# A decoder block on one core: the feed-forward entry written out in a fixed order with its weights split early, and the first score products shared

## The chip, the cores and the metric

The kernel runs on one core of a Trainium2 chip. The metric is device time in microseconds (us). Five engines run side by side, each with its own instruction stream: PE (TensorE, matmuls and transposes), ACT (ScalarE), DVE (VectorE), POOL (GpSimd) and SP (SyncE, which here issues nearly all DMAs). Semaphores tie them together. An engine works its stream in order, so an instruction that waits holds up all that stands behind it.

## The reference, cut to what matters

One decoder block on 512 tokens of width 1024: a norm, one combined projection, sparse attention beside an mLSTM, an output projection, and a feed-forward part with hidden width 4096. All in float32. The change touches the attention scores of the selected and of the window branch, and the feed-forward part:

```
s_s = einsum('bqghd,bqgnkd->bqghnk', qc, k_sel) + bias_s    # selected branch
p_s = masked_softmax(s_s, dist_s >= 0)
s_w = einsum('bqghd,bkgd->bqghk', qc, kwc) + bias_w         # window branch
p_w = masked_softmax(s_w, mask_w)
...
x = x + mixed @ w_out[l]
h2 = rms_norm(x, norm2_g[l])
x = x + square(relu(h2 @ w_ff1[l])) @ w_ff2[l]
```

With 512 tokens both branches see every earlier token, so the kernel computes both as causal attention over the whole sequence, with their own keys and values.

## The kernel before

**Matmuls in two halves.** A float32 operand is stored as a high part and a low part. `split` (L119) makes them: ACT writes the high part, then DVE subtracts it from the source and writes the low part. `mm3` (L114) multiplies them with three matmuls: high by high (L115), high by low (L116), low by high (L117). So every operand passes ACT and then DVE before its product can end.

**Attention.** There are 16 units: 8 heads, two branches each. `Unit.scores(qt)` multiplies 128 queries with their 128·(qt+1) keys, high and low part. For qt = 0 the product is 256 columns wide though 128 keys are needed. DVE then adds the bias and takes the row's extreme (`P`), and ACT takes the exponential. Work on the other branch (the "fill" stream) stands between these steps on PE. Once, between units, `cmp_scores(1)` (products `sc`, copied by ACT to `sT`, transposed to `sct` on PE) stands there too.

**Feed-forward entry.** After `out_proj`, DVE adds the residual (`x`), POOL takes a root, DVE writes `hn`, and `norm2_T(tt)` transposes one tile of 128 tokens in 8 PE transposes into `tpn`; `normed_T` splits them into `hT_h` and `hT_l` and copies them whole into `hF`. The token tiles 0 and 1 are done within `out_proj`, 2 and 3 within the first products. `first_ff1` computes the hidden blocks f = 0 to 3 directly: for tokens 0 to 255 four blocks of 24 matmuls, then the same for tokens 256 to 511, 192 matmuls of 256 columns in all. Then come relu, square and the split into `u`.

**Pairs of blocks.** From f = 4 on, two blocks at a time are computed by seven products (`do1` to `do7` in `products`) of 12 matmuls each, in place of eight. They take sums of token parts (T1 to T4, made from `hF` by three subtractions in `tokens`, a fourth for T4) and sums of weight parts (the forms a, s, t, b, made from `w1r` through `w1s` on DVE and then split). The products accumulate in four PSUM banks X, Y, Z and W. `do1` writes X, and ACT copies it out (`p1`, in the tile `g2`); `do5` adds to X and must wait for that copy. `do2` to `do4` leave sums in `g2` and `hn` on DVE. The second feed-forward matrix is applied in units of three 512-column matmuls, which `merge` sets between the products.

**What sets the order.** PE's order is the order in which the code is written (a manual schedule). The order on ACT, DVE, POOL and SP is chosen by a scheduler from its own estimates. In `mix` the numbers are times in the PE stream at which an event (such as `norm2_T(3)`) is put in. Buffers in a pool are reused in turn: a DMA into a `w1raw` or `w1r` tile waits until the last reader of that buffer is done.

Of the kernel before, what the change touches and what calls it, by code (L numbers as in the profile page):

```python
# [52 lines left out]
def hybrid_block_kernel(  # L53
# [91 lines left out]
    def normed_T(hn, tt, tags, full=None):  # L145
        for k0 in (0, 4):
# [705 lines left out]
    class Unit:  # L852
# [7 lines left out]
        def scores(self, qt):  # L860
            h, br = self.h, self.br
            if qt == 0:
                if br == 0:
                    for hn in ((h, h + 1) if h == 0 else (h + 1,)):
                        if hn < H:
                            bts[hn] = load_bias(hn)
                self.l = wk.tile([128, TT], F32, name="l4", bufs=3)
                self.nx = wk.tile([128, TT], F32, name="nx", bufs=3)
# [4 lines left out]
            nc.tensor.matmul(st[:, :m], qv, ks[:, br, 0, self.g, :m], start=True, stop=False)  # L873
            nc.tensor.matmul(st[:, :m], qv, ks[:, br, 1, self.g, :m], start=False, stop=True)  # L874
            P = wk.tile([128, n], F32, name="P", tag=f"P{qt}", bufs=3)
            c0 = 384 - 128 * qt
            V.tensor_tensor_reduce(P, st[:, :n], bts[h][:, c0:c0 + n], -1.0, 3e38, ALU.add, ALU.min,  # L877
# [148 lines left out]
    with pool("ffa") as fa, pool("ffr") as fr, pool("ffu") as fu, pool("fft") as ft:  # L1026
        UB = 13
        us = {}

        def utile(name, dt=F32R):  # L1030
            return fu.tile([128, 2 * S], dt, name=name, tag="u", bufs=UB)

        def ev_u(f, r):

            u = utile("u").rearrange("p (a t) -> p a t", a=2)
# [4 lines left out]
        def load_first(f):  # L1040
            parts = []
            for k in (0, 4):
                raw = fr.tile([128, 4, 256], F32, name="w1raw", tag="raw", bufs=2)
                nc.sync.dma_start(raw, w_ff1[:, k:k + 4, 128 * f:128 * f + 256])
                h, l = (utile("w1" + c).rearrange("p (k c) -> p k c", k=4) for c in "hl")
# [4 lines left out]
        def first_ff1():  # L1050

            ws = [load_first(0), load_first(2)]
            ps_ = [acc("pj", ("pj", "o")[f // 2], 2) for f in range(4)]
            for hs in (slice(0, 256), slice(256, 512)):
                for f in range(4):
                    for k in range(KT):
                        mm3(ps_[f][:, hs], *ws[f // 2](k, slice(128 * (f % 2), 128 * (f % 2) + 128)),
                            hT_h[:, k, hs], hT_l[:, k, hs], k == 0, k == KT - 1)
                        yield 3 * 256 / 2400
# [8 lines left out]
        def tokens():  # L1068
# [5 lines left out]
            for i, t in ((2, b22), (1, b11), (3, b12)):  # L1074
                T[i] = [ft.tile([128, 4, 256], F32R, name=f"T{i}{c}") for c in "hl"]
                split(*T[i], t)
            V.tensor_sub(b21, b21, b22)

            T[4] = [hT_h[:, 0:4, lo_], hT_l[:, 0:4, lo_]]

        def tokens4():
            split(*T[4], hF[1][:, :, hi_])
# [9 lines left out]
        def w1_load(f, first=False):  # L1092
            if first:
                raw, ss = ([utile(n, F32).rearrange("p (k c) -> p k c", k=4) for _ in range(2)] for n in ("w1r", "w1s"))
# [27 lines left out]
        def products(f, w, nxt):  # L1122
# [70 lines left out]

        def w2_load(i):
            if i < len(tiles2) and tiles2[i] not in w2s:
                c, ch, f = tiles2[i]
                raw = fr.tile([128, 2, S], F32, name="w2r", tag="raw", bufs=2)
                nc.sync.dma_start(raw, w_ff2[:, 8 * c + f:8 * c + f + 2, 512 * ch:512 * ch + 512])
                h, l = (fa.tile([128, 2, S], F32R, name="w2" + n, bufs=2) for n in "hl")
# [32 lines left out]
        def first_pair():  # L1232
            w = w1_load(4, first=True)
# [60 lines left out]
```

## Time and profile before

| | us |
|---|---|
| three runs | 810.63 to 811.78, median 811.16 |
| profiled execution | 809.97 |
| its span | 808.2 |
| PE busy | 787.5 (97%) |
| DVE busy | 536.3 (66%) |
| ACT busy | 407.3 (50%) |

The span is what the profile covers; 1.77 us of the profiled execution lie outside it. The profiled execution is 1.19 us below the median of the runs. A row of the timeline gives the start of an instruction, its length, its engine, its line and its operands; matmuls overlap in the pipeline, so what a matmul costs is the distance from its start to the next start, not its length.

### The profile page before, as it was taken

The page shows a single profiled execution, that of the slowest core. Times are in us where ns is not written, and L with a number is a line of the kernel's source. Part 1 is how long each engine was busy: PE and PEld are TensorE (multiplying, and loading weights), DVE is VectorE, ACT ScalarE, POOL GpSimd, SP SyncE. Part 2 cuts the span into 40 slices and gives each one's busy share as a digit, 9 for nine tenths or more (in the row PEclk, how much of TensorE's full clock was granted, in tenths as well). Part 3 has the DMA queues.
Part 4 walks back from the last instruction along what each step waited for, and adds up shares of the span by engine and source line. Part 5 has one row for each costly group of instructions (what it writes and reads, how often), then busy time and mean ns, then how long its engine had stood idle before and what let it go on. Part 6 is the DMA issues. An engine that isn't in the chain of part 4 may idle for free.

```text
span 808.2 us, 12445 instructions
## 1 busy us (share of the span) xinstructions
PE 787.5 (97%) x4772; PEld 697.3 (86%) x4772; DVE 536.3 (66%) x1007; ACT 407.3 (50%) x746; POOL 71.4 (9%) x150
## 2 busy tenths in 40 slices
PE   6999999999999999999999989999999999999998
PEld 5978889998888888888888789999998999989886
DVE  6689796778676657764754588677665767664332
ACT  6556564554466656664423576445444444444311
POOL 2000000322122221321000000000000000000000
PEclk9999999999999999999999999999999999999999
DMA  8633231666132123212332241423233333331141
GB/s 308 195 105 92 65 105 49 191 209 182 53 92 79 52 67 92 65 53 79 124 135 68 65 157 56 137 95 105 83 101 105 105 105 105 105 105 53 53 153 56
DMA packets 66320, 84.91 MB, mean 105 GB/s; under 512 B 4063, under 2 KB 50471, under 8 KB 66132
## 3 DMA queue, kind: packets, MB, share of 16 engines
q1 hardware_dynamic: 66168, 84.03, 33.2%
q8 instruction: 37, 0.61, 0.3%
q14 instruction: 23, 0.19, 0.1%
q10 hardware_dynamic: 92, 0.09, 0.0%
HBM read 81.98 MB, written 4.75 MB: 107 GB/s over the span
## 4 chain that ended last, share of the span: by engine, by line
PE 89%; DMA 4%; DVE 3%; ACT 2%; issue 1%; POOL 1%; SPq 0%; DVEq 0%; ACTq 0%; POOLq 0%
PE pj L115 18%; PE pj L116 18%; PE pj L117 18%; PE fo L115 7%; PE fo L117 7%; PE fo L116 7%; PE ao L911 3%; PE tpP L894 2%; PE st L874 1%; PE st L873 1%; DMA bt<-rel_d 1%; DMA w2r<-in_w_ff_dram 1%; PE tpn L149 1%; PE mo L431 1%; PE mo L430 1%
## 5 line engine op out<-in xcount | busy, mean ns | idle before, releaser
L115 PE MATMUL fo<-w2h,u 128*128 128x512 f32 x256 | 100.9, 394 | 0.0
L117 PE MATMUL fo<-w2h,u 128*128 128x512 f32 x256 | 100.2, 391 | 0.0
L116 PE MATMUL fo<-w2l,u 128*128 128x512 f32 x256 | 100.0, 391 | 0.0
L115 PE MATMUL pj<-whi,hT_h 128*128 128x256 f32 (+2 forms) x288 | 84.3, 293 | 3.5 <-ACT hT_h L120 1.8
L105 DVE TENSOR_TENSOR wlo<-wraw,whi 128x1024 fp32r<-128x1024 f32 (+2 forms) x58 | 72.1, 1243 | 21.7 <-ACT whi L104 20.7
L117 PE MATMUL pj<-whi,hT_l 128*128 128x256 f32 (+2 forms) x288 | 82.2, 286 | 0.0
L116 PE MATMUL pj<-wlo,hT_h 128*128 128x256 f32 (+2 forms) x288 | 81.9, 284 | 0.0
L115 PE MATMUL pj<-hT_h,whi 128*128 128x512 f32 x192 | 80.7, 420 | 0.4 <-DVE vv L121 0.4
L116 PE MATMUL pj<-hT_l,whi 128*128 128x512 f32 x192 | 75.9, 395 | 0.0
L117 PE MATMUL pj<-hT_h,wlo 128*128 128x512 f32 x192 | 75.7, 395 | 0.0
L104 ACT CAST whi<-wraw 128x1024 fp32r<-128x1024 f32 (+2 forms) x58 | 60.9, 1050 | 27.9 <-PE pj L116 12.7
L121 DVE TENSOR_TENSOR w2l<-w2r,w2h 128x1024 fp32r<-128x1024 f32 x32 | 39.2, 1223 | 50.1 <-ACT w2h L120 50.1
L120 ACT ACTIVATE w2h<-w2r 128x1024 fp32r<-128x1024 f32 x32 | 33.9, 1060 | 60.9 <-PE fo L117 60.9
L115 PEld LDWEIGHTS pj<-whi,hT_h 128*128 128x128 f32 x288 | 55.1, 191 | 5.0 <-ACT hT_h L120 2.1
L117 PEld LDWEIGHTS fo<-w2h,u 128*128 128x128 f32 x256 | 48.1, 188 | 11.1
L116 PEld LDWEIGHTS pj<-wlo,hT_h 128*128 128x128 f32 x288 | 55.2, 192 | 0.1
L117 PEld LDWEIGHTS pj<-whi,hT_l 128*128 128x128 f32 x288 | 55.0, 191 | 0.1
L116 PEld LDWEIGHTS fo<-w2l,u 128*128 128x128 f32 x256 | 48.3, 189 | 6.6
L115 PEld LDWEIGHTS fo<-w2h,u 128*128 128x128 f32 x256 | 48.2, 188 | 6.6
L877 DVE CUSTOM_DVE_ANT_0 P<-st,bt 128x128 f32<-128x128 f32 (+1 forms) x64 | 31.1, 486 | 28.5 <-PE st L874 26.2
L120 ACT ACTIVATE ph<-tpP 128x512 fp32r<-128x512 f32 (+1 forms) x64 | 27.8, 435 | 43.2 <-PE tpP L894 42.6
L887 POOL TENSOR_SCALAR P<-P,l 128x128 f32<-128x128 f32 (+1 forms) x64 | 34.2, 553 | 110.5 <-DVE l L885 110.5
(334 smaller groups left out, 2111.7 us busy)
## 6 DMA issues: line engine op xcount, KB each, us to landing
wraw<-in_w_in_dram SPq DMA_DIRECT2D x38, 512.0 KB, 3.8
w2r<-in_w_ff_dram SPq DMA_DIRECT2D x32, 512.0 KB, 3.7
w1r<-in_w_ff_dram SPq DMA_DIRECT2D x28, 512.0 KB, 4.8
bt<-rel_d SPq DMA_DIRECT2D x16, 256.0 KB, 2.9
wraw<-in_w_out_dram SPq DMA_DIRECT2D x8, 512.0 KB, 3.7
rel_d<-rel_r SPq DMA_DIRECT2D x1, 2560.0 KB
x<-in_x_dram SPq DMA_DIRECT2D x4, 512.0 KB, 8.2
wraw<-in_cmp_k_w_dram SPq DMA_DIRECT2D x8, 256.0 KB, 3.5
```

What stands on the lines that cost most here:

```text
L104: nc.scalar.copy(hi[:, :n], raw[:, :n])
L105: nc.vector.tensor_sub(lw[:, :n], raw[:, :n], hi.bitcast(F32)[:, :n])
L115: nc.tensor.matmul(o, ah, bh, start=start, stop=False, **kw)
L116: nc.tensor.matmul(o, ah, bl, start=False, stop=False, **kw)
L117: nc.tensor.matmul(o, al, bh, start=False, stop=stop, **kw)
L120: nc.scalar.activation(h, src, AF.Copy, scale=scale)
L121: nc.vector.tensor_sub(l, src, h.bitcast(F32))
L149: nc.tensor.transpose(tp[:, k * 128:(k + 1) * 128], hn[:, (k0 + k) * 128:(k0 + k + 1) * 128], ident)
L877: V.tensor_tensor_reduce(P, st[:, :n], bts[h][:, c0:c0 + n], -1.0, 3e38, ALU.add, ALU.min, self.nx[:, qt:qt + 1])
L887: nc.gpsimd.tensor_scalar(self.P[i], self.P[i], self.l[:, i:i + 1], 1.0, op0=ALU.mult, op1=ALU.mult)
L894: nc.tensor.transpose(tp[:, (qt - kt) * 128:(qt - kt + 1) * 128], self.P[qt][:, kt * 128:(kt + 1) * 128], ident)
L911: nc.tensor.matmul(o[:, S - x_.shape[-1]:], vn[:, self.br, self.g, kt, :], x_, start=self.br == 0 and kt == 0 and i == 0, stop=False)
```

## The change

It has two parts.

First, the score products of qt = 0 are shared. The product was 256 columns wide with 128 of use; now the selected branch's unit multiplies the queries with the first 128 keys of both branches at once, and the window branch's unit has no product for qt = 0. The part behind the product becomes a function, `soft`; for the window branch it is called at once, with the selected branch's, four steps earlier than before.

Second, the feed-forward entry. The raw weights for f = 0 to 3 and the weights of the first pair (f = 4) get buffers of their own and are loaded and split ahead of the products; `normed_T` copies the transposes whole to `hF` first and splits from that copy; the first block of `first_ff1` runs its 16 products with the high weights before its 8 with the low weights; `norm2_T(3)` stands 24 matmuls or so earlier in PE's stream; token sums, token forms and weight forms are events between the matmuls; w1's forms a and s for the next pair move from `do3` to `do4`; a load and a split of w2 are separate calls; the first pair is merged with 6 units from `do5` on, the second with 10. From here to the end of the first pair, ACT and DVE too run in the order in which the code is written.

```diff
-            split(hT_h[sl], hT_l[sl], tp.rearrange("p (k t) -> p k t", k=4))
+            t = tp.rearrange("p (k t) -> p k t", k=4)
             if full is not None:
-                nc.scalar.copy(full[k0 // 4][:, :, sl[2]], tp.rearrange("p (k t) -> p k t", k=4))
+                f = full[k0 // 4][:, :, sl[2]]
+                nc.scalar.copy(f, t)
+                t = f
+            split(hT_h[sl], hT_l[sl], t)
...
+            if qt == 0 and br == 1:
+                return
...
+            for i in range(2):
+                kv = ks[:, :, i, self.g, :n] if qt == 0 else ks[:, br, i, self.g, :n]
+                nc.tensor.matmul(st[:, :m], qv, kv, start=i == 0, stop=i == 1)
+            self.soft(qt, st[:, :n])
+            if qt == 0:
+                us[2 * h + 1].soft(qt, st[:, n:m])
...
+                    if f or hs.start:
+                        for k in range(KT):
+                            mm3(o, *wk_[k], hT_h[:, k, hs], hT_l[:, k, hs], k == 0, k == KT - 1)
+                            yield 3 * 256 / 2400
+                    else:
+                        for k in range(KT):
+                            nc.tensor.matmul(o, wk_[k][0], hT_h[:, k, hs], start=k == 0, stop=False)
+                            nc.tensor.matmul(o, wk_[k][0], hT_l[:, k, hs], start=False, stop=False)
+                            yield 2 * 256 / 2400
+                        for k in range(KT):
+                            nc.tensor.matmul(o, wk_[k][1], hT_h[:, k, hs], start=False, stop=k == KT - 1)
+                            yield 256 / 2400
...
             def do3():
                 prod(Z, "s1", 1, True)
                 V.tensor_add(t5, Z, u2)
+
+            def do4():
+                prod(W_, "t3", 3, True)
+                V.tensor_add(r[:, 1, lo_], W_, t5)
                 if w:
                     w1_a(w)
                     w1_s(w)
-
-            def do4():
-                prod(W_, "t3", 3, True)
-                V.tensor_add(r[:, 1, lo_], W_, t5)
...
-                for j in range(i, i + 2):
-                    w2_load(j)
+                w2_load(i + 2)
+                w2_split(i + 1)
...
-        mix(Stream(first_ff1()), [(1.54, lambda: norm2_T(2)), (7.32, after_norm), (11.0, first_pair),
-                                  (21.0, lambda: load_next(6)), (21.1, tokens4)])
+        ws = [load_first(0), load_first(2)]
+        w4 = w1_load(4, [tile4k("w1s", False, F32).rearrange("p (k c) -> p k c", k=4) for _ in range(2)]
+                     + [raw4k("w1r") for _ in range(2)])
+        ET = mybir.EngineType
+        es_start = ExitStack()
+        es_start.enter_context(tc.manual_schedule(engines={ET.PE, ET.Activation, ET.DVE}))
+        mix(Stream(first_ff1(ws)),
+            [(1.54, lambda: norm2_T(2)), (2.0, do((w1_a, w4), (w1_s, w4))),
+             (6.4, lambda: norm2_T(3)), (8.0, do((token_sums,), (token_form, 2), (token_form, 1))),
+             (12.0, do((w1_t, w4), (token_form, 3))), (15.6, do((w1_b, w4), (w2_load, 0), (w2_load, 1))),
+             (21.0, do((load_next, 6), (token_form, 4)))])
...
+                if lead and i == 2:
+                    w2_split(0)
...
-        merge((4, 6), 16, 3)
+        merge((4,), 6, 4)
+        es_start.close()
+        merge((6,), 10)
```

SP, from `out_proj`'s last weight loads on: `w1raw` are the raw weights for f = 0 to 3, `xr` the residual input, `w1r` the raw weights of the pair f = 4. Before:

```order
L103 DMA wraw_4953<-in_w_out_dram 128x2x512 [waits DMAHW7_49,DMAHW4_49,DVE_49]
L1044 DMA w1raw_5163<-in_w_ff1_dram 128x4x256
L1044 DMA w1raw_5169<-in_w_ff1_dram 128x4x256 [waits DMAHW1_49,DVE_49]
L1001 DMA xr_4881<-in_x_dram 128x512 [waits DMAHW2_49,DVE_49]
L1001 DMA xr_4911<-in_x_dram 128x512 [waits DVE_49]
L1001 DMA xr_4965<-in_x_dram 128x512 [waits DMAHW2_49,DVE_49]
L103 DMA wraw_4959<-in_w_out_dram 128x2x512 [waits DMAHW5_49,DVE_49]
L1001 DMA xr_5002<-in_x_dram 128x512 [waits DMAHW6_49,DMAHW3_49,DVE_49]
L1001 DMA xr_5039<-in_x_dram 128x512 [waits DMAHW7_49,DMAHW4_49,DVE_49]
```

After:

```order
L103 DMA wraw_4929<-in_w_out_dram 128x2x512 [waits DMAHW7_49,DMAHW4_49,DVE_49]
L1063 DMA w1raw_5139<-in_w_ff1_dram 128x4x256 [waits PE_49]
L1063 DMA w1raw_5145<-in_w_ff1_dram 128x4x256 [waits DMAHW1_49]
L1063 DMA w1raw_5151<-in_w_ff1_dram 128x4x256 [waits DMAHW2_49,DMAHW0_49,DVE_49]
L1063 DMA w1raw_5157<-in_w_ff1_dram 128x4x256 [waits DMAHW1_49,DVE_49]
L1016 DMA xr_4857<-in_x_dram 128x512 [waits DVE_49]
L1016 DMA xr_4887<-in_x_dram 128x512 [waits DMAHW5_49,DVE_49]
L1128 DMA w1r_5165<-in_w_ff1_dram 128x4x256 [waits DMAHW6_49,DMAHW2_49,DVE_49]
L1128 DMA w1r_5166<-in_w_ff1_dram 128x4x256 [waits DMAHW7_49,DMAHW3_49,DVE_49]
L1016 DMA xr_4941<-in_x_dram 128x512 [waits DMAHW4_49,DVE_49]
```

All four `w1raw` loads and the first pair's `w1r` loads now stand among the `xr` loads of `out_proj`; before, two of the four stood behind the last `xr`.

ACT, from the relu of block f = 2 on (before) and from the high part of form b on (after): `hn` with L1062 or L1091 is the relu of a block of `first_ff1`, `u` its high part, `hT_h<-hF` the high part of T4, `g2<-pj` the copy p1 of the bank X. Before:

```order
L1062 ACTIVATE hn_5445<-pj_5189 128x512 [waits DVE_49,PE_49]
L1036 ACTIVATE hn_5445<-hn_5445 128x512 [waits Activation_49]
L120 ACTIVATE u_5447<-hn_5445 128x512 [waits Activation_49]
L120 ACTIVATE T2h_5295<-hF_5052 128x1024 [waits DVE_49]
L1062 ACTIVATE hn_5475<-pj_5190 128x512 [waits DVE_49,PE_49]
L1145 COPY g2_5491<-pj_5487 128x256 [waits PE_49]
L1036 ACTIVATE hn_5475<-hn_5475 128x512 [waits Activation_49]
L120 ACTIVATE hT_h_83<-hF_5052 128x4x256 [waits DVE_49]
```

After:

```order
L120 ACTIVATE fbh_5397<-w1r_5166 128x1024 [waits DMAHW7_49]
L1091 ACTIVATE hn_5426<-pj_5173 128x512 [waits DVE_49,PE_49]
L1055 ACTIVATE hn_5426<-hn_5426 128x512 [waits Activation_49]
L120 ACTIVATE u_5428<-hn_5426 128x512 [waits Activation_49]
L1091 ACTIVATE hn_5456<-pj_5174 128x512 [waits DVE_49,PE_49]
L1055 ACTIVATE hn_5456<-hn_5456 128x512 [waits Activation_49]
L120 ACTIVATE u_5458<-hn_5456 128x512 [waits Activation_49]
L120 ACTIVATE hT_h_83<-hF_5028 128x4x256 [waits DVE_49]
L1174 COPY g2_5473<-pj_5469 128x256 [waits PE_49]
L120 ACTIVATE w2h_5514<-w2r_5401 128x1024 [waits DMAHW4_49,DMAHW3_49,DMAHW5_49,DMAHW2_49,DMAHW0_49]
```

The copy p1 stood one row behind the last relu and ahead of T4's high part; now it stands behind that block's square, its `u` and T4's high part, which waits for DVE.

DVE, at the change from the pair f = 4 to the pair f = 6: `u_5604`, `u_5634` (before) and `u_5614` (after) are low parts of f = 4's results, `fbl` is the low part of form b for f = 6, which `do5` of f = 6 reads, `g2_5653` and `g2_5637`, `hn_5638` belong to the products of f = 6. Before:

```order
L1176 TENSOR_TENSOR hn_5492<-pj_5490,g2_5491 128x256 [waits PE_49]
L121 TENSOR_TENSOR u_5604<-hn_5492,u_5604 128x512 [waits Activation_49]
L121 TENSOR_TENSOR fbl_5639<-w1r_5481,fbh_5638 128x1024 [waits Activation_49]
L121 TENSOR_TENSOR u_5634<-hn_5492,u_5634 128x512 [waits DVE_49,Activation_49]
L1149 TENSOR_TENSOR g2_5653<-pj_5650,g2_5653 128x256 [waits PE_49]
L1115 TENSOR_TENSOR w1s_5643<-w1r_5642 128x4x128 [waits DMAHW3_49]
L121 TENSOR_TENSOR fal_5704<-w1r_5642,fah_5703 128x512 [waits Activation_49]
```

After:

```order
L121 TENSOR_TENSOR w2l_5687<-w2r_5554,w2h_5686 128x1024 [waits DMAHW1_49,Activation_49]
L1178 TENSOR_TENSOR g2_5637<-pj_5634,g2_5637 128x256 [waits DVE_49,Activation_49]
L1182 TENSOR_TENSOR g2_5637<-pj_5635,g2_5637 128x256 [waits DVE_49,PE_49]
L1186 TENSOR_TENSOR hn_5638<-pj_5636,g2_5637 128x256 [waits DVE_49,PE_49]
L121 TENSOR_TENSOR u_5614<-hn_5474,u_5614 128x512 [waits Activation_49]
L121 TENSOR_TENSOR fbl_5619<-w1r_5462,fbh_5618 128x1024 [waits Activation_49]
L1144 TENSOR_TENSOR w1s_5623<-w1r_5622 128x4x128 [waits DMAHW4_49]
```

The low part of form b stood ahead of the first sum of f = 6's products; now it stands behind three of them, the last of which (`hn_5638`) needs `do4` of f = 6.

## Rows read from the trace of the kernel before

Each row stands as the profile gives it; times are microseconds from the start of the span unless marked ns. Within a group, a line of dots stands for rows left out.

**Rows 1.** The page: busy time (part 1); the chain by engine (part 4)

```profile
PE 787.5 (97%) x4772; PEld 697.3 (86%) x4772; DVE 536.3 (66%) x1007; ACT 407.3 (50%) x746; POOL 71.4 (9%) x150
...
PE 89%; DMA 4%; DVE 3%; ACT 2%; issue 1%; POOL 1%; SPq 0%; DVEq 0%; ACTq 0%; POOLq 0%
```

**Rows 2.** PE timeline, 456 to 489: start, duration, engine line op [idle<-releaser]

```profile
456.67 0.40 PE L117 MATMUL pj<-whi,mx_l 128*128 128x512 f32 x1
...
458.98 0.39 PE L117 MATMUL pj<-hT_h,w1l 128*128 128x256 f32 x1 [1.21 <-DVE w1l L121]
...
468.71 1.04 PE L149 MATMUL tpn<-ident,hn 128*128 128x128 f32 x8
469.50 0.36 PE L115 MATMUL pj<-hT_h,w1h 128*128 128x256 f32 x1
...
472.65 0.28 PE L117 MATMUL pj<-hT_h,w1l 128*128 128x256 f32 x1
...
475.35 0.39 PE L116 MATMUL pj<-hT_l,w1h 128*128 128x256 f32 x1 [1.74 <-DVE hT_l L121]
...
475.69 0.32 PE L115 MATMUL pj<-hT_h,w1h 128*128 128x256 f32 x1
...
479.22 0.28 PE L117 MATMUL pj<-hT_h,w1l 128*128 128x256 f32 x1
...
488.18 0.28 PE L115 MATMUL pj<-hT_h,fah 128*128 128x256 f32 x1
```

**Rows 3.** Windows: length, busy by engine, PEclk, DMA share, GB/s

```profile
457.00:459.00 2.00, 0.59 (x4) 0.32 (x3) 1.89 (x3) 1.33 (x4) 0.00 (x0) 1.00 0.00 0
...
476.00:477.00 1.00, 1.00 (x7) 1.00 (x6) 1.00 (x2) 0.99 (x3) 0.00 (x0) 0.50 0.07 16
```

**Rows 4.** Timeline of PE, 240.8 to 241: one pair of score products

```profile
240.84 0.28 PE L873 MATMUL st<-ks,qy 128*128 128x256 f32 x1
240.96 0.28 PE L874 MATMUL st<-ks,qy 128*128 128x256 f32 x1
```

**Rows 5.** Timeline of ACT, 309 to 315

```profile
309.15 0.39 ACT L879 ACTIVATE P<-P,nx 128x128 f32<-128x128 f32 x1
...
314.25 0.58 ACT L814 COPY sT<-sc 128x512 f32<-128x512 f32 x1
```

**Rows 6.** Timeline of PE, 314.8 to 315

```profile
314.88 0.66 PE L820 MATMUL sct<-ident,sT 128*128 128x128 f32 x4
```

**Rows 7.** Timeline of DVE, 420 to 421

```profile
420.28 0.69 DVE L1007 SCALAR_TENSOR_TENSOR x<-pj,xr 128x512 f32<-128x512 f32 x1 [5.71 <-PE pj L117]
```

**Rows 8.** Timeline of PE, 421.4 to 421.6

```profile
421.48 0.40 PE L115 MATMUL pj<-whi,mx_h 128*128 128x512 f32 x1
```

**Rows 9.** Timeline of SP, 413 to 414

```profile
413.02 1.02 SPq L1044 DMA_DIRECT2D w1raw<-in_w_ff_dram  x2
```

**Rows 10.** The page, DMA issues (part 6): KB each, us to landing

```profile
w1r<-in_w_ff_dram SPq DMA_DIRECT2D x28, 512.0 KB, 4.8
```

**Rows 11.** Timeline of DVE, 460 to 462: the norm of token tile 3

```profile
460.74 1.41 DVE L143 SCALAR_TENSOR_TENSOR hn<-x,nr,g 128x512 f32<-128x512 f32 x2
```

**Rows 12.** Timeline of ACT, 479 to 490

```profile
479.89 0.60 ACT L1062 ACTIVATE hn<-pj 128x512 f32<-128x512 f32 x1 [2.31 <-PE pj L117]
...
481.73 1.04 ACT L120 ACTIVATE T1h<-hF 128x1024 fp32r<-128x1024 f32 x1
...
489.79 0.37 ACT L1145 COPY g<-pj 128x256 f32<-128x256 f32 x1 [0.82 <-PE pj L117]
```

**Rows 13.** Timeline of DVE, 478 to 496

```profile
478.68 1.22 DVE L1071 TENSOR_TENSOR hF<-hF 128x1024 f32<-128x1024 f32 x1
...
482.09 0.68 DVE L121 TENSOR_TENSOR u<-hn,u 128x512 fp32r<-128x512 f32 x1
...
495.22 0.41 DVE L1149 TENSOR_TENSOR g<-pj,g 128x256 f32<-128x256 f32 x1
```

More of the change, by code (lines that the diff above doesn't have):

```diff
@@ L872, in scores, with soft @@
             qv = qs[h // 2][:, h % 2, qt * 128:(qt + 1) * 128]
[L873 to L875 removed]
+            for i in range(2):
[4 more added lines that the diff above has]
+                us[2 * h + 1].soft(qt, st[:, n:m])
+        def soft(self, qt, st):
+            h, br = self.h, self.br
+            n = 128 * (qt + 1)
+            if qt == 0:
+                self.l = wk.tile([128, TT], F32, name="l4", bufs=4)
+                self.nx = wk.tile([128, TT], F32, name="nx", bufs=4)
+            P = wk.tile([128, n], F32, name="P", tag=f"P{qt}", bufs=4 if qt == 0 else 3)
             c0 = 384 - 128 * qt
[L877 removed]
+            V.tensor_tensor_reduce(P, st, bts[h][:, c0:c0 + n], -1.0, 3e38, ALU.add, ALU.min,
                                    self.nx[:, qt:qt + 1])
@@ L1019, in hybrid_block_kernel, with tile4k, raw4k @@
     es_ring.close()
-    with pool("ffa") as fa, pool("ffr") as fr, pool("ffu") as fu, pool("fft") as ft:
-        UB = 13
+    with pool("ffa") as fa, pool("ffw") as fw, pool("ffv") as fv, pool("fft") as ft:
         us = {}
-        def utile(name, dt=F32R):
-            return fu.tile([128, 2 * S], dt, name=name, tag="u", bufs=UB)
+        def tile4k(name, first, dt=F32R):
+            p_, n = (fw, 8) if first else (fv, 5)
+            return p_.tile([128, 2 * S], dt, name=name, tag="u", bufs=n)
+        def raw4k(name):
+            return fw.tile([128, 4, 256], F32, name=name, tag="raw", bufs=2)
         def ev_u(f, r):
-            u = utile("u").rearrange("p (a t) -> p a t", a=2)
+            u = tile4k("u", (f + 8) % 13 < 8).rearrange("p (a t) -> p a t", a=2)
             nc.scalar.activation(r, r, AF.Square)
@@ L1042, in load_first @@
             for k in (0, 4):
-                raw = fr.tile([128, 4, 256], F32, name="w1raw", tag="raw", bufs=2)
+                raw = raw4k("w1raw")
                 nc.sync.dma_start(raw, w_ff1[:, k:k + 4, 128 * f:128 * f + 256])
-                h, l = (utile("w1" + c).rearrange("p (k c) -> p k c", k=4) for c in "hl")
+                h, l = (tile4k("w1" + c, True).rearrange("p (k c) -> p k c", k=4) for c in "hl")
                 split(h, l, raw)
@@ L1073, in tokens, with token_form @@
             V.tensor_sub(b22, b22, b11)
[L1074 to L1082, printed above, removed]
+        def token_form(i):
+            if i == 4:
+                V.tensor_sub(hF[1][:, :, hi_], hF[1][:, :, hi_], hF[1][:, :, lo_])
+                T[4] = [hT_h[:, 0:4, lo_], hT_l[:, 0:4, lo_]]
+            else:
+                T[i] = [(fa if (i, c) == (3, "h") else ft).tile([128, 4, 256], F32R, name=f"T{i}{c}") for c in "hl"]
+            split(*T[i], {1: hF[0][:, :, hi_], 2: hF[1][:, :, lo_], 3: hF[0][:, :, lo_], 4: hF[1][:, :, hi_]}[i])
         forms = {}
@@ L1090, in form, with w1_load @@
             forms[key] = h, l
-        def w1_load(f, first=False):
-            if first:
-                raw, ss = ([utile(n, F32).rearrange("p (k c) -> p k c", k=4) for _ in range(2)] for n in ("w1r", "w1s"))
+        def w1_load(f, tiles=None):
+            if tiles:
+                ss, raw = tiles[:2], tiles[2:]
             else:
@@ L1192, in hybrid_block_kernel, with w2_split @@
         tiles2 = [(c, ch, f) for c in range(4) for ch in range(2) for f in range(0, 8, 2)]
+        w2r = {}
         def w2_load(i):
-            if i < len(tiles2) and tiles2[i] not in w2s:
+            if i < len(tiles2):
                 c, ch, f = tiles2[i]
-                raw = fr.tile([128, 2, S], F32, name="w2r", tag="raw", bufs=2)
+                w2r[i] = raw = raw4k("w2r").rearrange("p (f k) c -> p f (k c)", f=2)
                 nc.sync.dma_start(raw, w_ff2[:, 8 * c + f:8 * c + f + 2, 512 * ch:512 * ch + 512])
-                h, l = (fa.tile([128, 2, S], F32R, name="w2" + n, bufs=2) for n in "hl")
+        def w2_split(i):
+            if i < len(tiles2):
+                raw = w2r.pop(i)
+                h, l = (t.tile([128, 2, S], F32R, name="w2" + n, bufs=2) for t, n in ((fa, "h"), (ft, "l")))
                 split(h, l, raw)
```

25 lines of the change are left out of this document (9 added, 16 removed).

## Prediction

> **What bounds the kernel now.** I read the page first: PE is busy for 97% of the span, and 89% of the chain that ended last is PE [rows 1]. So time comes from two sources only: fewer or shorter matmuls, and less waiting on PE. The timeline of PE then shows where it waits; nearly all of it lies at the feed-forward entry [rows 2]. The last matmul of the output projection starts at 456.67. At about 0.12 us for 256 columns [rows 4] and twice that for 512, the first product could start at 456.90. The first of its matmuls that needs a low weight starts only at 458.98, released by DVE. A second stop begins at 472.65: the matmul that needs the low part of token tile 3 starts at 475.35, again released by DVE. Then the granted clock is 0.50, the lower of the two levels (1.2 GHz), in the second window [rows 3]: from 475.69 to 479.22 PE starts 17 matmuls in 3.53 us, where full speed takes 17 × 0.118 = 2.01. That costs 1.52. In the first window, with the first stop, it is 1.00. The first matmul of `do1` starts at 488.18. The work between is 192 matmuls × 0.118 = 22.66 and two groups of 8 transposes at 469.50 − 468.71 = 0.79 each, 24.24 together, so it could start at 481.14. All stops of the entry together, the low clock among them, cost 488.18 − 481.14 = 7.04. This is the largest gain open to the change.
>
> **Shared score products.** Eight heads lose one pair of 256-column products each, 16 × 0.118 = **−1.89** [rows 4]. All of it is on the path, since PE has no wait there. No other work is removed: the second half of the product was computed before and thrown away.
>
> What is moved is the softmax step of the window branch for qt = 0: one step on DVE and one on ACT (0.39 on ACT [rows 5]) come four steps earlier. This is free as long as ACT and DVE have slack. At one place they have none: `sT` is copied by ACT from 314.25 to 314.83 [rows 5], and the transposes that read it start at 314.88 [rows 6]. Just ahead of it the two extra steps now stand in the chain from `P` over `ay` and `qy` to `sT`. Bounds: nothing, if the copy slips ahead; two steps of 0.39, so 0.8, if both lie in the chain. I take **+0.7**, near the upper end, because the rows leave 0.05 of slack.
>
> **Weights loaded and split early.** All four `w1raw` loads now go out in `out_proj`, and their splits (ACT 1.04, DVE 1.22 each [rows 12, 13]) lie under matmuls there. ACT and DVE have room. What can be hurt is the residual add: on DVE it stands behind the low half of the second `w1raw`. Before, this add ran from 420.28 to 420.97 [rows 7], and the bank that it frees was wanted at 421.48 [rows 8], so there is 0.51 of slack. The two loads were issued between 413.02 and 414.04 [rows 9]; with the 4.8 us of such a load [rows 10] the second lands at about 418.5, its split ends at about 420.8, the add at about 421.5, just as the bank is wanted. Bounds: 0, and one split late, 1.2. I take **+0.3**. The `xr` loads that stand behind on SP wait for buffers that come free with these adds anyway.
>
> **First blocks at full rate.** With low weights at hand, the first stop goes (458.98 less 456.90 and two matmuls, 1.84). For token tile 3, `hn` is written by DVE from 460.74 to 462.15 [rows 11]; its transposes move from 468.71 to about 464.8, after 64 matmuls less the earlier stops. One copy and two splits later, its last low half is ready at about 468.7 (ACT 0.6 and DVE 0.68 a step, one step held by form s). The first half of the products ends at about 469.85. So the second stop goes too, and with it the low clock: `do1` starts at 481.14, **−7.04**. That is counted as if the entry started at 456.90 as before; the terms above shift it as a whole.
>
> **What is late next.** This is the point of the change. The preparation of the pair is one chain over ACT and DVE, and it is now in written order. I add it up with the rows' prices [rows 12, 13]: 1.22 for 1024 elements on DVE (1.25 where each waits for the one before; 1.14 back to back), 1.04 on ACT, 1.84 from one relu to the next row behind its square and `u` (479.89 to 481.73), 0.37 for the copy p1.
> From 468.7: three dependent subtractions, 472.45. T2 high, 473.5. T2 and T1 low, 475.9. Two sums of weights, 477.1. Form t high and T3 high, 479.1. Then four blocks of relu, square and `u` with the high part of form b between, 4 × 1.84 + 0.95, 487.4. The last `u` low and the fourth subtraction on DVE, 489.4. T4 high, 490.5. And only then, behind it on ACT, the copy p1: 490.85.
> PE meanwhile: `do1` and `do2` at 1.42 each end at 484.0. `do3` needs the bank of block 2, whose relu ends at 484.4: +0.40. `do4` needs that of block 3: +0.45. `do5` is wanted at 487.7, but it adds to the bank that p1 is copied from: it waits until 490.87, **+3.17**. Before, that copy ran right after `do1` (489.79, one row behind the last relu [rows 12]).
> Behind p1 on ACT stands the high half of the first w2 tile, and on DVE its low half stands behind T4's low half and two sums (0.41 each [rows 13]): about 493.75. PE wants it after `do5` and one matmul, 492.5: +1.25.
> In the next pair (f = 6), form b's low half now stands on DVE behind the sum of `do4`: 0.42 + 0.60 + 1.22 and hops, 2.4 us after `do4`, where PE has one unit (0.70) and two matmuls (0.24) to run: +1.46. Bounds 0 and 2.4. That low half also frees the buffer of the raw weights of f = 8. The load takes 4.8 [rows 10], two sums and form s 3.6 more, other DVE work in between some 1.8: 12.6 us after `do4`, where PE has 11.3 to run: +1.27. Bounds 0 and 2.
> Sum: 0.40 + 0.45 + 3.17 + 1.25 + 1.46 + 1.27 = **+8.0**.
>
> **The clock.** PE now runs about 5 of the 10 us from 484 to 494. After the stop from 472.65 (2.70 with two matmuls in it) the rows of before show 1.52 lost to the low clock; after the one of 1.84 none [rows 2, 3]. The wait for w2 swallows most of it, because a slower `do5` only ends later inside that wait. Bounds 0 and 1.52; I take **+0.4**. The Trainium skill, "TensorE: Matmul & The Clock Gate", section "🎯 Why this matters for your kernels", says to keep PE from idling between bursts of matmuls, or it falls back to the lower clock. By it the stop ahead of `do5` would cost the full 1.52, and the sum would be 1.1 higher. The trace of before agrees for the stop at 472.65 and shows nothing for the shorter one.
>
> **Sum.** −1.89 + 0.7 + 0.3 − 7.04 + 8.0 + 0.4 = +0.47. The profiled execution took 809.97, so 810.44; it was 1.19 below the median of the runs, so I forecast **811.6** against 811.16: no change that can be measured. I call 0.2%, 1.6 us, the least that can be told from no change.
>
> **Rivals.** *The low clock stays* (slower). The place is `do5`; it decides if the clock falls while PE waits there and stays low past 494, and again after the wait at w2: two stretches as before cost 3.0, of which the wait for w2 takes back 1.25, so 1.75 in place of 0.4, about 813.0. For it: the stop of before that was shorter than this one brought the clock down. Against it: PE's work in the first units after `do5` is dense.
> *The later feeds are in time* (faster). If the low half of form b and the raw weights of f = 8 arrive before PE asks, as they did before the change, 2.73 goes, and without the low clock 0.4 more: 808.5. For it: the two terms are small differences of long sums, and from f = 6 on ACT and DVE again run in the scheduler's order. Against it: the row of form b does stand behind the sum of `do4`.
> *The whole gain* (faster). If `do5` doesn't wait, all of 7.04 and 1.89 stay, about 803 to 804. Against it: the order on ACT is fixed, and p1 stands behind T4.
> *A late front* (slower): both front terms at their upper ends, +1.0, with 0.6 of the clock: 813.2.
>
> **How the numbers follow.** Forecast 0.48 (809.6 to 812.8); later feeds in time 0.18; whole gain 0.04; low clock stays 0.2; late front 0.1. Of the forecast's own case little falls outside 0.2%. So faster 0.22, same 0.48, slower 0.30. The range reaches from the later feeds in time, with a little of the front terms gone too, 808.2, to the low clock with one front term at its end, 814.0.
>
> **What would show it.** The profile after should have PE without stops until `do3`, `do1` about 7 us earlier after the last matmul of the output projection, token tile 3's low half before the second half of the products wants it; a stop of about 3 us ahead of `do5`, released by ACT, with the copy p1 right behind T4's high part; a stop of about 1.2 ahead of the first unit's second matmul, released by DVE; one of about 1.5 in `do5` of f = 6 and one in `do2` of f = 8; a wait ahead of `sct` near 314. The prediction is wrong if `do5` waits much less or more than 3 us, or if a stop appears where I have none, above all in `out_proj`.

## The result, and the profile after

The changed kernel takes 815.92 us in the median of six runs (814.05 to 817.35) against 811.23 for the kernel before. The ratio is 1.0053, with a 95% interval of 1.0035 to 1.0071: slower. The forecast was 811.6, and its range ended at 814.0, so the time lies outside it.

The page of the profiled execution (817.09 us, the second longest of the six; span 815.3) answers to [rows 1]. PE's share of the chain fell from 89% to 80%, and DVE, DMA and ACT took it.

```profile
PE 788.7 (97%) x4756; PEld 697.1 (86%) x4756; DVE 537.0 (66%) x1007; ACT 407.3 (50%) x746; POOL 71.8 (9%) x150
...
PE 80%; DVE 7%; DMA 6%; ACT 4%; issue 2%; POOL 0%; SPq 0%; ACTq 0%; DVEq 0%; POOLq 0%
```

The timeline of PE at the entry and behind it answers to [rows 2]. The first matmul of the feed-forward part, the transposes of token tile 3, `do1`, `do5`, the second matmul of the first unit, `do5` of f = 6, and two matmuls in `do2` of f = 8:

```profile
458.20 0.28 PE L1083 MATMUL pj<-hT_h,w1h 128*128 128x256 f32 x1
...
466.08 1.03 PE L149 MATMUL tpn<-ident,hn 128*128 128x128 f32 x8
...
482.50 0.28 PE L115 MATMUL pj<-hT_h,fah 128*128 128x256 f32 x1
...
491.68 0.38 PE L115 MATMUL pj<-hT_h,fbh 128*128 128x256 f32 x1 [2.84 <-ACT g L1174]
...
494.68 0.79 PE L116 MATMUL fo<-w2l,u 128*128 128x512 f32 x1 [0.65 <-DVE w2l L121]
...
514.75 0.39 PE L117 MATMUL pj<-hT_h,fbl 128*128 128x256 f32 x1 [1.32 <-DVE fbl L121]
...
525.84 0.39 PE L115 MATMUL pj<-T2h,fsh 128*128 128x256 f32 x1 [1.23 <-ACT fsh L120]
...
527.42 0.58 PE L117 MATMUL pj<-T2h,fsl 128*128 128x256 f32 x1 [1.08 <-DVE fsl L121]
```

In the text a stop is the distance between two starts less what the first instruction takes at full clock (0.118 for 256 columns, 0.234 for 512), so it is 0.1 to 0.4 longer than the idle time in the brackets. No stop lies between 458.20 and `do1`: the entry runs at full rate, as forecast. Behind it the long stops that the prediction named are there, with the releasers that it named, where it named one; ahead of `do3` there is none, and ahead of `do4` 0.28. ACT shows why for `do5`: T4's high part waits for DVE, and the copy p1 stands behind it (to compare with [rows 12]).

```profile
490.31 1.06 ACT L120 ACTIVATE hT_h<-hF 128x1024 fp32r<-128x1024 f32 x1 [1.89 <-DVE hF L1106]
491.28 0.35 ACT L1174 COPY g<-pj 128x256 f32<-128x256 f32 x1
491.53 1.06 ACT L120 ACTIVATE w2h<-w2r 128x1024 fp32r<-128x1024 f32 x1
```

Ahead of the entry there are three stops that the kernel before does not have, at the `sct` transposes [rows 6], at the bank that the residual add frees [rows 8], and at a low weight of the output projection:

```profile
315.19 0.66 PE L823 MATMUL sct<-ident,sT 128*128 128x128 f32 x4 [0.64 <-ACT sT L817]
...
421.91 0.50 PE L115 MATMUL pj<-whi,mx_h 128*128 128x512 f32 x1 [0.67 <-DVE x L1022]
...
438.36 0.50 PE L116 MATMUL pj<-wlo,mx_h 128*128 128x512 f32 x1 [0.53 <-DVE wlo L105]
```

And the clock falls twice, from 492.9 to 499.8 and from 527.1 to 530.5 (windows as in [rows 3]: PEclk is the third column from the end):

```profile
493.00:494.00 1.00, 1.00 (x5) 0.51 (x3) 0.94 (x2) 0.11 (x1) 0.00 (x0) 0.50 0.00 0
498.00:499.00 1.00, 1.00 (x7) 1.00 (x6) 0.93 (x1) 1.00 (x3) 0.00 (x0) 0.50 0.00 0
528.00:529.00 1.00, 1.00 (x7) 1.00 (x6) 1.00 (x2) 0.99 (x3) 0.00 (x0) 0.50 1.03 338
```

One table makes all kernels of this study comparable. I divide each profiled execution at three matmuls: a transpose `tph` near 202 us, the first feed-forward matmul, and the first matmul of `do1`. The stretch before `tph` is the same code in all of them and varied from 201.4 to 204.4 between executions, so it is left out of every comparison of stages. Part of the variation goes with the clock: six of the executions have some 3.4 us at 0.50 between 168 and 189 (the second profile of the changed kernel, `ff_only`, `t4_late`, `w4_early`, `w4_cmp` and `stop1`), the others none there. It is not all of it: `s_only`, with 203.54, has none.

| kernel | to `tph` | to the first ff matmul | to `do1` | to the end | median of runs |
|---|---|---|---|---|---|
| before | 201.99 | 255.28 | 30.91 | 320.02 | 811.2 |
| changed | 202.69 | 255.51 | 24.30 | 332.80 | 815.92 |
| changed, second profile | 203.28 | 255.54 | 24.36 | 331.12 | (816.07, one run) |
| s_only | 203.54 | 254.33 | 32.30 | 320.03 | 810.75 |
| ff_only | 204.39 | 258.04 | 24.30 | 327.17 | 813.92 |
| t4_late | 203.74 | 256.11 | 24.30 | 332.25 | 817.22 |
| busy24 | 202.18 | 255.48 | 24.30 | 326.24 | 811.58 |
| close_early | 202.06 | 256.33 | 24.30 | 323.51 | 808.62 |
| w4_early | 203.86 | 257.28 | 24.31 | 319.75 | 804.87 |
| w4_cmp | 202.80 | 255.24 | 24.31 | 319.75 | 803.79 |
| w4_cmp_again | 201.44 | 255.64 | 24.30 | 319.82 | 803.48 |
| w4_pool | 202.97 | 257.89 | 24.37 | 319.77 | 807.42 |
| stop1 | 201.99 | 255.44 | 24.30 | 321.67 | 804.93 |
| stop3 | 202.71 | 255.08 | 24.30 | 323.21 | 809.58 |

The change won 6.6 us in the third column and lost 11 to 13 in the fourth.

### The profile page after: what moved, and what is told of

It reads as the page before. It is cut to its first block, busy times and chain, and to the rows that moved or that the text cites. A ratio compares the mean times of both kernels' runs of the same rounds, so it can differ in the third digit from the quotient of the medians.

```text
span 815.3 us, 12402 instructions
## 1 busy us (share of the span) xinstructions
PE 788.7 (97%) x4756; PEld 697.1 (86%) x4756; DVE 537.0 (66%) x1007; ACT 407.3 (50%) x746; POOL 71.8 (9%) x150
## 4 chain that ended last, share of the span: by engine, by line
PE 80%; DVE 7%; DMA 6%; ACT 4%; issue 2%; POOL 0%; SPq 0%; ACTq 0%; DVEq 0%; POOLq 0%
PE pj L115 16%; PE pj L116 16%; PE pj L117 16%; PE fo L115 7%; PE fo L116 7%; PE fo L117 7%; PE ao L926 2%; DMA wraw<-in_w_in_dram 2%; PE st L879 2%; PE tpP L909 2%; DVE wlo L105 1%; DMA w1r<-in_w_ff_dram 1%; ACT whi L104 1%; DMA w1raw<-in_w_ff_dram 1%; PE mo L434 1%
## 5 line engine op out<-in xcount | busy, mean ns | idle before, releaser
L892 DVE CUSTOM_DVE_ANT_0 P<-st,bt 128x128 f32<-128x128 f32 (+3 forms) x64 | 30.6, 487 | 26.7 <-PE st L879 23.4
```

Of the source, the lines that this page charges most:

```text
L892: V.tensor_tensor_reduce(P, st, bts[h][:, c0:c0 + n], -1.0, 3e38, ALU.add, ALU.min, self.nx[:, qt:qt + 1])
```

## The experiments

**One part of the change at a time.** `s_only` is the kernel before with only the shared score products; `ff_only` is the changed kernel with the score products of before.

> Only the shared score products; the feed-forward part as before. Theory (the sharing is worth what the rows say): 16 matmuls less, -1.89, and a stop of 0.8 ahead of the sct transposes near 315, so 810.1, 1.1 below before. Rival (the sharing costs more elsewhere, for instance it is what puts PE 0.7 us behind by 202): 810.8 to 811.5, with stops or a late start that before does not have.

> Only the feed-forward part of the change; the score products as before. Theory (the two parts add up): 1.1 above the changed kernel, about 817.0, with the stops of 0.8 and 0.7 in out_proj, 3.0 ahead of do5, 1.5 in do5 of f=6, 2.6 in do2 of f=8, and the clock at 0.50 twice. Rival (the stops in out_proj come from the shifted scores): 815 to 816, and no stops near 422 and 438.

`s_only`: 0.9995 of before (0.9986 to 1.0004). The theory does not fit. The products and the `sct` stop (0.80 again) are worth about what was said: 0.95 less up to the first feed-forward matmul. But the entry behind it grew by 1.39, a cost elsewhere as the rival has it in general, though not the one that it names. There ACT's order held: the high part of token tile 3 stands behind the high part of form b, whose load had not landed. That order and a wait for that load are in the kernel before too. Counted from `tph`, form b's load went out 0.5 earlier in `s_only`, but landed 6.7 us after its issue in place of 5.8, so PE, arriving earlier, only waited longer. Why the load took longer is not shown. ACT, then PE, in `s_only`:

```profile
473.66 1.06 ACT L120 ACTIVATE fbh<-w1r 128x1024 fp32r<-128x1024 f32 x1 [0.87 <-DMA w1r<-in_w_ff_dram]
474.62 1.06 ACT L120 ACTIVATE hT_h<-tpn 128x512 fp32r<-128x512 f32 x2
```

```profile
475.25 0.38 PE L115 MATMUL pj<-hT_h,w1h 128*128 128x256 f32 x1 [1.75 <-ACT hT_h L120]
```

`ff_only`: 1.0043 of before (1.0029 to 1.0056), so by the medians about 2 us below the changed kernel, not 1.1 above it, though the two intervals overlap. The stops in `out_proj` are there without the shared scores, so the rival falls too. In the profiles the difference lies behind `do1` (327.17 against 332.80): in `do2` of f = 8 it stopped only once, for 0.8, and the clock did not fall there. What differs is the time that a load took, told below with the second profile of the changed kernel.

**T4 behind do3.**

```diff
-             (21.0, do((load_next, 6), (token_form, 4)))])
+             (21.0, do((load_next, 6),))])
...
                 if lead and i == 2:
+                    token_form(4)
                     w2_split(0)
```

> The changed kernel with T4 made behind do3 instead of ahead of do1, so that the copy p1 stands ahead of T4's high part on ACT; the first w2 tile's split stays behind T4. Theory (one chain over ACT and DVE feeds do5 and then the first unit): the stop ahead of do5 falls from 3.0 to 0.2 and a stop of about 3 appears ahead of the first unit, beside the 1.1 at its second matmul; time within 1 us of the changed kernel, about 815.5, and the clock falls all the same. Rival (p1's place alone is the cause): 3 us and the low clock go, 810 to 812.5.

Measured: 817.22, 1.0077 of before (1.0063 to 1.0092), no better than the changed kernel. The stop moved as the chain theory says. `do5` ran on time, and the first unit waited, because w2's high part stands behind T4 on ACT. PE, then ACT:

```profile
490.37 0.39 PE L115 MATMUL pj<-hT_h,fbh 128*128 128x256 f32 x1
...
494.87 0.73 PE L115 MATMUL fo<-w2h,u 128*128 128x512 f32 x1 [2.81 <-ACT w2h L120]
```

```profile
489.96 0.35 ACT L1174 COPY g<-pj 128x256 f32<-128x256 f32 x1
492.81 1.06 ACT L120 ACTIVATE hT_h<-hF 128x1024 fp32r<-128x1024 f32 x1 [2.49 <-DVE hF L1106]
493.77 1.04 ACT L120 ACTIVATE w2h<-w2r 128x1024 fp32r<-128x1024 f32 x1
```

Taking one wait away from such a chain gives it to the next reader.

**Work in the stop.**

```diff
             def do5():
+                if f == 4:
+                    dm = acc("dm", "s", 2)
+                    for i in range(24):
+                        nc.tensor.matmul(dm[:, :256], T[1][0][:, i % 4, 0:128], T[1][0][:, i % 4, :],
+                                         start=i == 0, stop=i == 23)
                 prod(X, "b1", 21, False)
```

> The changed kernel with 24 extra matmuls of 256 columns on PE between do4 and do5, into a bank that nobody reads (2.83 us of work inside the stop of 3.0; all else as changed). Theory (the stop ahead of do5 brings the clock down, and that costs about 3 us up to 499.6): granted clock 1.00 from 493 on, 3 us below the changed kernel, about 813. Rival 1 (the clock falls for the wait at w2 and the thin work behind it): clock still falls, time as the changed kernel, 815 to 816.5. Rival 2 (the low clock costs little, as forecast): within 0.5 of the changed kernel.

Measured: 1.0006 of before (0.9995 to 1.0017): with 2.83 us of useless work more, the kernel is 4.3 us faster than the changed one. The granted clock was 1.00 throughout in the profiled execution, and its mean was 0.998 or more in all twelve runs. From the first matmul of `do5` to the first of `do7` PE took 498.20 − 491.13 = 7.07 here and 501.04 − 491.68 = 9.36 in the changed kernel, where the stop at w2 was even shorter.

```profile
488.13 3.04 PE L1195 MATMUL dm<-T1h 128*128 128x256 f32 x24
491.13 0.38 PE L115 MATMUL pj<-hT_h,fbh 128*128 128x256 f32 x1
...
494.13 0.50 PE L116 MATMUL fo<-w2l,u 128*128 128x512 f32 x1 [1.09 <-DVE w2l L121]
...
498.20 0.28 PE L115 MATMUL pj<-hT_h,fbh 128*128 128x256 f32 x1
```

So the low clock cost 2.3 us in that stretch. The rest of the gain is not the first stretch: the scheduler, seeing 24 matmuls more, put form s ahead of form b for f = 8, and the stops in `do2` of f = 8 and the second low clock were gone as well. This run mixes the two.

**Where the written order ends.** `close_early` closes the fixed order of ACT and DVE behind the first blocks. `w4_early` also asks for the four weight forms of f = 4 ahead of that order, and takes them out of the events of `mix` (not shown):

```diff
+        for g in (w1_a, w1_s, w1_t, w1_b):
+            g(w4)
         ET = mybir.EngineType
         es_start = ExitStack()
...
+        es_start.close()
         n2 = iter(order2)
...
         merge((4,), 6, 4)
-        es_start.close()
```

> The changed kernel with the fixed order of ACT and DVE ending at the last matmul of the first blocks, so that from do1 on the scheduler orders them again. Theory (the written order behind the first blocks makes the stops, and the low clock follows the stops): the stops at do5, w2, f=6 and f=8 go (8.2 us in the changed kernel), smaller ones of 1 to 2 us each come ahead of do2 to do4 (about 4.5), the low clock costs 0 to 2 in place of 3.7; 809.5 to 812.5. Rival (the feeds are late whatever the order, because ACT and DVE have too much to do there): 814 to 816.

> As close_early, and the weight forms a, s, t, b of the pair f=4 are asked for ahead of the fixed order, so that ACT and DVE can make them within out_proj, where they have room. Theory (the chain of 22 us between token tile 3 and do5 is what makes PE stop; four forms less in it bring it under PE's work): no stop over 0.3 and no low clock from the first feed-forward matmul on; 8.4 and 3.7 us less than the changed kernel, 803.8, and below the kernel before. Rival (the load of the forms moves the stop into out_proj): stops in out_proj grow by 2 or more; 806 to 808.

`close_early`: 0.9976 of before (0.9966 to 0.9987), 808.62, better than the theory's range. Two stops are left, 1.58 and 1.76, both for a relu that frees a bank; neither is as long as the 3.00 of the changed kernel, the clock stayed at 1.00 in this profiled execution, and f = 6 and f = 8 were fed in time.

```profile
487.35 0.39 PE L115 MATMUL pj<-T1h,fsh 128*128 128x256 f32 x1 [1.43 <-ACT hn L1091]
...
490.65 0.39 PE L115 MATMUL pj<-T3h,fth 128*128 128x256 f32 x1 [1.60 <-ACT hn L1091]
```

`w4_early`: 0.9926 (0.9913 to 0.9940), 804.87. No stop over 0.3 is left behind the first feed-forward matmul; the last column of the table is 319.75, as good as before, and the gain of the entry is kept. Its rival is half right, though: in its profiled execution the way to the first feed-forward matmul is 1.8 longer than in the changed kernel, with four stops of 0.7 to 1.0 in `out_proj`.

**The front.** `w4_cmp` moves `cmp_scores(1)` and its transposes one step on:

```diff
-            if (u, i) == (8, 0):
+            if (u, i) == (8, 1):
                 sT = cmp_scores(1)
-            if (u, i) == (8, 1):
+            if (u, i) == (8, 2):
                 pc = cmp_soft(1, sT)
```

`w4_pool` gives the low halves of the first blocks' weights to POOL on top of that (`nc.gpsimd.tensor_sub(l, raw, h.bitcast(F32))` in `load_first`).

> As w4_early, with cmp_scores(1) and the transposes behind it one step later, away from the two softmax steps. Theory (the shared products lose 0.8 only at the sct transposes): that stop goes, 0.8 below w4_early. Rival (the stop moves on with them): no difference beyond 0.3.

> As w4_cmp, with the low halves of the first blocks' weights made by POOL in place of DVE. Theory (the stops near 422 and 438 come from these splits standing ahead of the residual add on DVE): both stops go, 1 to 1.5 below w4_cmp. Rival (POOL is too slow or disturbs DVE): a stop at the first low weights, or no gain.

`w4_cmp`: 0.9915 (0.9902 to 0.9928), 803.79; once more, with five runs, 0.9911 (0.9898 to 0.9925), 803.48. The stop at `sct` is gone, at the price of 0.32 at a later transpose. The medians differ from `w4_early` by 1.1, more than these two make; the intervals overlap, so the exact gain is not resolved. This is the best kernel of the study, 7 us below the kernel before.

> The same kernel as w4_cmp, as the base of the two runs that follow: 803.8, no stop over 0.35 and a granted clock of 1.00 from the first feed-forward matmul on. A rival that would spoil the base: the gain came from that one chip, and the kernel is within 0.3% of the one before.

`w4_pool`: 0.9959 (0.9944 to 0.9973), 3.6 above `w4_cmp`. The stop at the residual add went, as the theory says: on DVE the add was now free. But one split took 2.41 on POOL against 1.23 on DVE, and the raw buffers came free later: the loads for f = 4 went out at 428.18 and 431.41, against 425.47 and 428.63 in `w4_cmp`. So the second of them stood just ahead of the last weights of the output projection (issued at 432.50, against 432.25), and ACT could start on these only at 437.31, against 435.82. That the two loads slow each other is my reading; no run separates them. PE stopped there instead (1.79 and 1.02), and the clock fell behind it, as a window shows:

```profile
438.40 0.50 PE L115 MATMUL pj<-whi,mx_h 128*128 128x512 f32 x1 [1.63 <-ACT whi L104]
439.66 0.79 PE L116 MATMUL pj<-wlo,mx_h 128*128 128x512 f32 x1 [0.76 <-DVE wlo L105]
```

```profile
440.00:441.00 1.00, 1.00 (x3) 0.81 (x3) 0.00 (x0) 0.00 (x0) 0.00 (x0) 0.50 0.00 0
```

**The price of a stop by itself.** In `w4_cmp`, which has no long stop, one is made in `do5` of f = 12 (`stop1` with one pass of POOL):

```diff
                 V.tensor_add(r[:, 1, lo_], W_, t5)
+                if f == 12:
+                    bl = forms["b"][1].rearrange("p k c -> p (k c)")[:, :512]
+                    nc.gpsimd.tensor_scalar(tmp[:, 3], r[:, 1, lo_], 0.0, 1.0, op0=ALU.mult, op1=ALU.add)
+                    for i in range(3):
+                        nc.gpsimd.tensor_scalar(bl, bl.bitcast(F32), tmp[:, 3, 0:1], 1.0, op0=ALU.mult, op1=ALU.mult)
```

> w4_cmp with one stop of PE made on purpose: ahead of do5's low weights at f=12, POOL passes over half of form b's low part three times, multiplied by one, after do4's sum, so that PE waits about 3.3 us; nothing else is moved that PE waits for. Theory (such a stop brings the clock down and costs 2 to 2.5 us beyond its length): 5.3 to 5.8 above w4_cmp, granted clock 0.50 for some 3 to 6 us behind it. Rival (the forecast's price: a stop costs its length and about 0.4): 3.3 to 3.8 above w4_cmp.

> As stop3 with one pass of POOL in place of three, a stop of about 1.8 us. Theory (the price beyond the length comes with the clock only, which did not fall after the stop of 1.84 in the kernel before): 1.8 above w4_cmp and a granted clock of 1.00. Rival (every stop costs more than its length): 2.5 or more above w4_cmp.

PE in `stop3`, with the windows behind its stop, then PE in `stop1`:

```profile
563.17 0.39 PE L117 MATMUL pj<-hT_h,fbl 128*128 128x256 f32 x1 [3.19 <-POOL fbl L1191]
```

```profile
563.00:565.00 2.00, 1.83 (x13) 1.74 (x14) 0.00 (x0) 0.34 (x1) 0.12 (x1) 1.00 0.00 0
565.00:567.00 2.00, 2.00 (x15) 1.82 (x14) 0.00 (x0) 0.99 (x2) 0.00 (x0) 1.00 0.04 8
```

```profile
561.23 0.38 PE L117 MATMUL pj<-hT_h,fbl 128*128 128x256 f32 x1 [1.61 <-POOL fbl L1191]
```

`stop1` (a stop of 1.76) took 804.93, 1.45 more than its base: its length, no more. `stop3` (3.34) took 809.58 in the median of twelve runs, 6.1 more than its base: its length and 2.8. But its runs lie from 806.84 to 811.13, that is 3.4 to 7.7 above the base. The profiled one was among the shortest, and in it the clock did not fall at all. So neither theory holds for every execution: a stop of this length costs from its bare length to more than twice it. No long run of this kernel was profiled, but the mean granted clock of every run is on record, and it goes with the time: the three runs at 0.999 took 806.84 to 807.13, the nine at 0.995 to 0.998 took 808.08 to 811.13. Of the sixteen runs of `w4_cmp`, `w4_cmp_again` and `stop1` only two are below 0.998. So the clock fell in most runs of `stop3`, and not in all.

**The changed kernel once more.**

> The changed kernel once more, one look. If the second stop in do2 of f=8 (2.6) belongs to the order, it is there again with about the same size; if it hangs on when the raw weights land (5.7 us after their issue in the first profile, 3.7 in ff_only), it is 0.8 to 1.3 where they land early, and the second stretch of low clock near 528 is then missing. Time 814 to 817.4.

816.07. `do5` waited 3.00 again and `do2` of f = 8 stopped for 1.62 and 1.24, so this stop belongs to the kernel. The low clock came earlier this time, and for half as long: it lay from 492.6 to 496.0, most of it within `do5`. The two matmuls at w2 start 0.43 apart, which is what 512 columns take at the low clock, so the wait there was all but gone: it had swallowed most of the low clock, as forecast. From `do5` to `do7` PE took 7.35. Two windows of this profile follow its PE rows.

```profile
492.36 0.43 PE L115 MATMUL pj<-hT_h,fbh 128*128 128x256 f32 x1 [2.84 <-ACT g L1174]
...
499.71 0.28 PE L115 MATMUL pj<-hT_h,fbh 128*128 128x256 f32 x1
...
524.68 0.39 PE L115 MATMUL pj<-T2h,fsh 128*128 128x256 f32 x1 [1.45 <-ACT fsh L120]
...
526.26 0.39 PE L117 MATMUL pj<-T2h,fsl 128*128 128x256 f32 x1 [1.08 <-DVE fsl L121]
```

```profile
493.00:494.00 1.00, 1.00 (x7) 1.00 (x6) 0.90 (x3) 0.78 (x2) 0.00 (x0) 0.50 0.00 0
498.00:499.00 1.00, 1.00 (x8) 0.88 (x7) 0.26 (x1) 1.00 (x3) 0.00 (x0) 1.00 0.21 82
```

The DMA view of the load for f = 8 goes with the size of the second stop. The changed kernel (514 to 521.5), then `ff_only` (516 to 523); the last column of the issue row is us to landing. Under each stands the row of DVE's first reader of this load, with its wait:

```profile
q8 instruction: 1, 0.02, 1.8%
...
w1r<-in_w_ff_dram SPq DMA_DIRECT2D x2, 512.0 KB, 6.7
```

```profile
520.42 0.69 DVE L1144 TENSOR_TENSOR w1s<-w1r 128x512 f32<-128x512 f32 x1 [5.73 <-DMA w1r<-in_w_ff_dram]
```

```profile
w1r<-in_w_ff_dram SPq DMA_DIRECT2D x2, 512.0 KB, 4.8
```

```profile
520.46 0.69 DVE L1132 TENSOR_TENSOR w1s<-w1r 128x512 f32<-128x512 f32 x1 [3.78 <-DMA w1r<-in_w_ff_dram]
```

The stops in `do2` of f = 8 grow nearly one for one with this time: 0.81 in all where the load landed in 4.8 (`ff_only`, the median of [rows 10]), 2.4 at 6.5 (`t4_late`), 2.63 at 6.7 and 2.86 at 6.9 (the changed kernel). DVE's wait for it, which ends 1.0 sooner in each, is the 3.7 and the 5.7 of the expectation. Why the load took longer stays open. In the three executions with the long load one packet of the instruction queue (q8) falls into it, in `ff_only` none does. But such a packet is not enough: in the changed kernel one falls into the load for f = 4 too (window 425.5 to 432), whose two halves went out 2.9 us apart, and that load landed in 3.8.

## Why the prediction was wrong

By the stages of the table the prediction said −1.3, −6.7 and +8.4, +0.5 in all. The second profile of the changed kernel, whose time is that of the median, has +0.3, −6.6 and +11.1. So of the 4.3 us between forecast and median 2.7 lie behind `do1` and 1.5 ahead of the entry. The remainder of the second profile's difference to the kernel before, 1.3, is the stretch ahead of `tph`, where this execution has a stretch of low clock (168.3 to 171.7) and the kernel before has none.

*Right.* The entry runs without a stop (24.30 where 24.24 was summed up). The chain over ACT and DVE and its end: p1 at 491.28 behind T4, a stop of 3.00 at `do5` (3.17 said), 1.06 at w2, part of it the low clock's (1.25), 1.48 at f = 6 (1.46), 0.80 at `sct` (0.7). `do3` and `do4` cost 0.28 in place of 0.85. `close_early` and `w4_early` confirm the mechanism: with the order given back the long stops go and two of 1.58 and 1.76 come in their place, and with four forms less in the chain on top of that these go too.

*The step that failed: the feed of f = 8 and the clock, summed at 1.27 and 0.4.* The mechanism of the feed was named, late form b, hence a late load. Its size was not: 2.63 and 2.86, since the load took 6.7 to 6.9 and not the 4.8 of the sum (with 4.8, in `ff_only`, the stop was 0.81), and two waits follow on each other, for the high part of form s, which stands behind form b's on ACT, and for its low part. The bound of 2 that I gave was too low. Behind this second long stop the clock fell again, which the sum didn't have at all: about 1.5 to 1.7 by the windows at 0.50 there. In `t4_late`, with 2.4 of stops there, it fell too; in `ff_only`, with 0.81, it did not. And the first low clock is not always swallowed by the wait at w2: it cost 2.3 in one profile and 0.3 in the other (9.36 and 7.35 against the 7.07 of `busy24`). The rival "the low clock stays" had two stretches, but both near `do5` and the wait at w2, none at f = 8; it put them at 1.75 with f = 8's price unchanged, and so ended at 813.0. The stage behind `do1` is 2.7 to 4.4 above the sum, nearly all of it these two. The runs on record agree on the clock's part: of the changed kernel's six, the three with a mean granted clock of 0.993 took 816.40 to 817.35, the three at 0.995 to 0.999 took 814.05 to 815.45. That even the run at 0.999 took 814.14 says that the clock alone is not the miss.

By the rule of the Trainium skill ("TensorE: Matmul & The Clock Gate", section "🎯 Why this matters for your kernels") that was weighed against the 0.4, PE was to be kept from idling between bursts of matmuls, or it falls back to the lower clock. `busy24` agrees: with the stop filled with work, the clock stayed at 1.00. The profiled run of `stop3` does not: its clock stayed at 1.00 after 3.34 us of waiting, so by these runs the fall is possible at each long stop, not certain.

*The front, said −0.9 and found +0.6 in both profiles.* (The table's column shows less, +0.2 and +0.3, since the kernel before waited 0.37 ahead of its first feed-forward matmul, 457.27 where 456.90 was possible, and the changed kernel does not.) The products gave 1.89 by their count and `sct` took 0.80, but the residual add cost 0.84 where 0.3 was taken, and 0.69 at 438 was not foreseen, a stop in `out_proj` of the kind that the prediction itself had called a sign of being wrong: the fourth split stands ahead of a residual add on DVE (427.57 and 428.71 in the changed kernel), ACT's square waits for that add, and the weights of the output projection wait behind the square. That is read from the trace; `w4_pool`, which took the splits off DVE, moved the loads with them and so does not test it alone; the cause stays argued. I had walked the first add, and not the later ones on the same engines.

*A smaller error of method:* the sum was set against a profiled execution that was 1.19 below the median of its runs, and I corrected for that; the stretch up to 202 us, which varies by 3 us between executions, can make such a difference by itself.

## What to carry to other kernels

A hand-written order over several engines moves a wait more easily than it removes one: count for each engine what stands ahead of the instruction that the bottleneck needs next, and let the order end where its reason ends. When PE runs at full rate, price each long stop at its length plus a possible fall of the clock, at every such stop and not only at the longest. And if a stop comes from a chain, moving one wait in it gained nothing here (`t4_late`); giving ACT and DVE their order back behind the first blocks gained 7.3 us by the medians, and making four weight forms earlier, where the two had room, 3.8 more.

## What the runs showed of the hardware

- The same 1 MB load for f = 8 landed in 6.5 to 6.9 us in three executions (both profiles of the changed kernel and `t4_late`) and in 4.8 in `ff_only`. A packet of the instruction queue fell into the three long ones; that it is the cause is not shown.
- The clock does not always fall after a stop of a given length: 0.50 after 2.5 us in the kernel before [rows 2, 3] and after 1.79 and 1.02 with one matmul between them in `w4_pool`, 1.00 after 3.34 in the profiled run of `stop3`, and 0.50 for 6.8 and for 3.4 us after the same stop of 3.00 in two profiles of the changed kernel.
- A stop of 3.34 us made on purpose (`stop3`) cost 3.4 to 7.7 us over twelve runs, and the runs with the lower mean granted clock are the longer ones. One of 1.76 (`stop1`) cost 1.45.
- A subtraction of 128x1024 that takes 1.23 us on DVE took 2.41 on POOL.
